# A feed-forward product split over two 64-row tiles of the tensor engine, with the halves exchanged after a drain

## The chip, the core and the metric

The kernel runs on one core of a Trainium2 chip. The core has five engines that run side by side, each with its own queue of instructions: TensorE (PE in the profile; its weight loads have a row of their own, PEld), VectorE (DVE), ScalarE (ACT), GpSimd (POOL) and SyncE (SP), which here starts the transfers. The metric is the time of one execution in device microseconds (us).

## What is computed

The reference is a block of two layers over 16 learned tokens and 256 input tokens with 1024 features. Each layer has a mixer (three branches: retention, a gated linear recurrence, and differential attention, with input projections, branch projections and an output projection) and then a feed-forward part with a short causal convolution. The change lies in the first product of the feed-forward part, `hn @ w_ffn_in`:

```python
def conv_ffn(hn, w_ffn_in, conv_w, conv_b, w_ffn_out, valid):
    u = jnp.where(valid[None, :, None], hn @ w_ffn_in, 0.0)
    up = jnp.pad(u, ((0, 0), (CONV_W - 1, 0), (0, 0)))
    c = conv_b + sum(conv_w[j] * up[:, j:j + l] for j in range(CONV_W))
    gate, val = jnp.split(c, 2, axis=-1)
    return (jax.nn.silu(gate) * val) @ w_ffn_out
```

`w_ffn_in` has 1024 rows and 5632 columns: 22 feature tiles of 128 for the gate and 22 for the value.

## The kernel before

**Layout.** Activations stand with features on the 128 partitions and tokens along the columns. A product takes a 128x128 tile of the weights as the loaded operand and all tokens as the moving one: 272 columns in the first layer, 258 in the second (`t0` is 0, then 14).

**Three products for one.** Each float32 operand is split into a rounded part and the rest, both of type `F32R` (the profile prints f32): `wh`, `wl` for weights, `hi`, `lo` for activations (tiles `xh`, `xl`). One tile of a product is `wh*hi + wh*lo + wl*hi`, lines 801, 802 and 803, each with a weight load of its own.

**`products` (line 780)** issues one pair of feature tiles. For `fi`, pair `j` is gate tile `j` and value tile `j+22`; `f` (0 or 1) says which of the two, and each accumulates in a PSUM bank of its own (`to[j, f]`). The eight row tiles `k` of the 1024 features are run through as k = 0 to 3, then 4 to 7, each with f = 0, then f = 1: 16 tiles, 48 matmuls. There are 22 such pairs in each of the two layers. The PSUM tile `main` has two buffers, so one pair can be emptied while the next is computed.

**Weights (`_Weights`, line 501)** come in chunks of eight tiles (512 KB): SP fetches `wraw` (3 buffers), ACT rounds it to `whi`, DVE takes the rest into `wlo` (4 buffers each), lines 524 to 526. A pair of `fi` uses two chunks, the first for k = 0 to 3, the second for k = 4 to 7. A chunk is asked for `LEAD` = 6 us ahead of its first use by the planner's clock.

**The planner.** Nothing is issued as it is written down. `plan.add` records an operation with its engine, an estimated cost and a key (a due time on `clock`, which the products advance); `_Plan.order` then simulates the engines and fixes the order of each queue by these costs, keys, dependencies and free buffers. In the code before, one planned operation is one tile (three matmuls). Real waits are semaphores set at the level of the instructions.

**Around the product.** The output projection `wo` runs before the first pair. While `fi` begins, the norm's factor is computed (a float32 matmul to `ms`, line 741, in pair 0), and the first four pairs are scaled by it when they are emptied (`evacuate`, DVE). From the fifth pair on (`DEFER`, `Norm.next`, line 750) the activations themselves carry the factor: the tiles for k < 4 go to a second set (`xs[2]`), those for k >= 4 are written again in place (`xs[1]`), with ACT writing `xh` and DVE writing `xl`. DVE and ACT also do the convolution of each pair (`two_b`), the gate and the split for the next product (`ghi`, `glo`). After the 22 pairs comes the second product `fo`.

**An existing place with 64 rows.** The attention scores (`da_head`, line 1176, tile `ds`) are float32 matmuls over 64 partitions: head part m = 0 on partitions 0 to 63, m = 1 on 64 to 127, issued in turn, into two PSUM banks.

```python
for q0, nk, at in tiles:
    for m in range(2):
        half = slice(64 * m, 64 * m + 64)
        nc.tensor.matmul(ss[m][:, at : at + nk], q[half, hd, q0 : q0 + P], k[half, hd, :nk], start=True, stop=True)
```

Of the kernel before, what the change touches and what calls it, by code (L numbers as in the profile page):

```python
# [25 lines left out]
KD = D // P  # L26
# [56 lines left out]
def _ktiles(name):  # L83
    return FK if name == "fo" else KD
# [462 lines left out]
def _trace(ctx, tc, plan, a, depth, probe):  # L547
    nc = tc.nc
    act = _Engine(plan, nc.scalar, "act", 0.094, 0.833e-3)
    dve = _Engine(plan, nc.vector, "dve", 0.068, 1.042e-3)  # L550
    pe = _Engine(plan, nc.tensor, "pe", 0.0, 4 / 2400)
# [12 lines left out]
    weights = _Weights(plan, wp, a["w"], act, dve, sync)  # L564
    serial = [0]

    def new(pool_, shape, dt, tag, bufs, name):
        serial[0] += 1
        return plan.tile(pool_, shape, dt, tag, bufs, f"{name}_{serial[0]}")

    def fixed(shape, name, dt=F32):
        return new(cp, shape, dt, name, 1, name)
# [86 lines left out]
    xs = [[fixed([P, KD // 2, T], f"x{n}{i}", F32R) for n in "hl"] for i in range(3)]  # L659

    def x_tile(k, folded):
        return tuple(t[:, k % 4, :] for t in xs[1 if k >= 4 else 2 if folded else 0])
# [113 lines left out]
    clock = [0.0]  # L776
# [3 lines left out]
    def products(xs, name, j, t0=0):  # L780

        if name in BASE or name == "fi":
            norm.next()
        if ahead:
            return ahead.pop()
        tiles = turns.pop(0)
        main = lambda: new(mp, [P, 2, 512], F32, "main", 2, "main")[:, :, t0:T]
        ps = {i: main() for i in sorted({x[1] for x in tiles})}
        to = {x: ps[x[0]][:, x[1], :] for x in {x[1::2] for x in tiles}}
        if (name, j) == ("fo", 3):  # L790

            to[j, 1] = main()[:, 1, :]
        cost = 3 * ((T - t0) / 2400 + 0.003)
        nk = _ktiles(name)
        for _, i, k, f in tiles:
            hi, lo = (x[:, t0:] for x in xs(k))
            plan.key = clock[0]
            wh, wl = weights.next()

            def run(o=to[i, f], wh=wh, wl=wl, hi=hi, lo=lo, first=k == 0, last=k == nk - 1):  # L800
                nc.tensor.matmul(o, wh, hi, start=first, stop=False)  # L801
                nc.tensor.matmul(o, wh, lo, start=False, stop=False)  # L802
                nc.tensor.matmul(o, wl, hi, start=False, stop=last)  # L803

            plan.main.append(plan.add("pe", run, cost, [to[i, f]], [wh, wl, hi, lo]))
            clock[0] += cost
        plan.key = clock[0] - 1.0
        if (name, j) == ("fo", 3):
            return [to[j, f] for f in range(2)]
        ahead.extend(ps[i] for i in ps if i != j)  # L810
        return ps[j]
# [64 lines left out]
    for li in range(depth):  # L876
# [4 lines left out]
        t0 = META - 2 if last else 0  # L881
# [453 lines left out]
        for name, j in ORDER:  # L1335
# [31 lines left out]
            if name in BASE:  # L1367
                lo = 0 if name in ("rk", "rv", "hf", "hi", "dk", "dv") else t0
                ps = products(lambda k: x_tile(k, norm.folded), name, j, lo)
                if name in ("rg", "hg", "m0", "m1", "m2"):  # L1370
                    if j == 0:
# [43 lines left out]
                else:  # L1415
# [6 lines left out]
                    if lo and j % 2:  # L1422
                        pool.memset(t[:, :, :lo], 0.0)
            elif name in ("b0", "b1", "b2"):
                ps = products(st["x" + name], name, j, t0)
                g = st["m" + name[1]][:, both, t0:]
                yy = block(f"y{j // 2}")[:, two, t0:]
# [10 lines left out]
            elif name == "wo":  # L1438
                hi, lo = st["yhi"], st["ylo"]
                ps = products(lambda k: (hi[k // 4][:, k % 4, :], lo[k // 4][:, k % 4, :]), name, j, t0)  # L1440
                tt(h[:, both, t0:], h[:, both, t0:], ps, ADD)
                if j == 0:
# [5 lines left out]
            elif name == "fi":  # L1448
                ps = products(lambda k: x_tile(k, norm.folded), name, j, t0)
# [9 lines left out]
                for f in range(2):  # L1459
                    ft = j + f * FK  # L1460
                    w = lambda i: small[:, S_CW + (li * 3 + i) * 2 * FK + ft : S_CW + (li * 3 + i) * 2 * FK + ft + 1]
# [12 lines left out]
            else:  # L1474
                hi, lo = st["ghi"], st["glo"]
                ps = products(lambda k: (hi[k // 4][:, k % 4, :], lo[k // 4][:, k % 4, :]), name, j)
# [34 lines left out]
```

## Time and profile before

| what | value |
|---|---|
| median of 2 runs | 1334.65 us (1334.08 to 1335.23) |
| the profiled execution | 1334.28 us, of which the span from first to last instruction is 1332.5 us |
| mean granted TensorE clock | 0.999 |
| matmuls, and as many weight loads | 11862 |
| matmuls of lines 801 to 803 into `main` from `xh`, `xl` | 2368 for each line |
| DVE, ACT busy | 72%, 61% of the span |

The profile is of one execution. Its rows give, for groups of instructions, the busy time, the mean duration of one, and what ended the idle time before them. Matmuls overlap in the pipeline, so the duration of one (some 290 ns) is longer than the distance from one start to the next; the distance is what a stream of matmuls costs. The end of a matmul is modelled.

### The profile page before, as it was taken

The numbers are of one execution on the slowest core, as the hardware profiler recorded it, in microseconds if no ns is written. First come the engines' busy times: TensorE is split into PE (matmuls) and PEld (weight loads), VectorE is DVE, ScalarE is ACT, GpSimd is POOL, SyncE is SP. The second block draws the span as 40 slices with busy tenths as digits, with TensorE's granted clock in tenths as the row PEclk, the third lists the DMA queues.
The fourth block names the chain that finished last, engine by engine and source line by source line (L and its number), as shares of the span: only waits on it lengthen the run. The fifth ranks groups of instructions, "written<-read, shape, count | busy, mean of one in ns | idle before, by whom it ended". The sixth has DMA issues, their size and how long they took to land.

```text
span 1332.5 us, 28912 instructions
## 1 busy us (share of the span) xinstructions
PE 1320.4 (99%) x11862; PEld 1292.5 (97%) x11862; DVE 961.9 (72%) x1628; ACT 813.2 (61%) x1371; POOL 84.2 (6%) x162
## 2 busy tenths in 40 slices
PE   9999999999999999999999999999999999999998
PEld 9999999999999999999999999999999999999986
DVE  7575777697676789886564757776985867898753
ACT  6747454756576567665446574557566775767643
POOL 5000000000010020000030000000011100200000
PEclk9999999999999999999999999999999999999999
DMA  7644543443544545555555545444445446466653
GB/s 269 192 142 156 164 160 128 139 147 127 175 143 157 176 152 174 183 174 176 177 177 180 161 151 167 161 128 144 143 152 169 143 156 203 143 206 189 196 186 109
DMA packets 60755, 219.07 MB, mean 164 GB/s; under 512 B 6864, under 2 KB 6992, under 8 KB 60624
## 3 DMA queue, kind: packets, MB, share of 16 engines
q1 hardware_dynamic: 60336, 216.71, 50.3%
q8 instruction: 93, 1.52, 0.5%
q10 hardware_dynamic: 288, 0.52, 0.1%
q14 instruction: 38, 0.31, 0.1%
HBM read 216.16 MB, written 1.05 MB: 163 GB/s over the span
## 4 chain that ended last, share of the span: by engine, by line
PE 94%; DVE 4%; issue 1%; DMA 1%; ACT 0%; SPq 0%; DVEq 0%
PE main L801 27%; PE main L802 27%; PE main L803 27%; PE fo L1311 2%; PE fo L1313 2%; PE fo L1312 2%; PE lev L992 1%; DVE two_b L496 1%; PE ds L1176 1%; DVE wlo L496 1%; PE ms L496 1%; PE do L496 1%; PE ro L496 1%; PE ho L496 1%; DVE xl L496 1%
## 5 line engine op out<-in xcount | busy, mean ns | idle before, releaser
L801 PE MATMUL main<-xh,whi 128*128 128x272 f32 (+1 forms) x2368 | 693.7, 293 | 1.8 <-ACT whi L496 1.1
L802 PE MATMUL main<-xl,whi 128*128 128x272 f32 (+1 forms) x2368 | 677.1, 286 | 2.4 <-DVE xl L496 2.4
L803 PE MATMUL main<-xh,wlo 128*128 128x272 f32 (+1 forms) x2368 | 677.0, 286 | 0.5 <-DVE wlo L496 0.4
L496 DVE TENSOR_TENSOR wlo<-wraw,whi 128x1024 fp32r<-128x1024 f32 (+1 forms) x406 | 496.4, 1228 | 204.5 <-ACT whi L496 201.3
L496 ACT ACTIVATE whi<-wraw 128x1024 fp32r<-128x1024 f32 (+1 forms) x406 | 426.3, 1052 | 235.4 <-PE main L802 165.1
L802 PEld LDWEIGHTS main<-xl,whi 128*128 128x128 f32 x2368 | 446.0, 188 | 3.5 <-DVE xl L496 3.0
L801 PEld LDWEIGHTS main<-xh,whi 128*128 128x128 f32 x2368 | 445.4, 188 | 3.5 <-ACT whi L496 1.3
L803 PEld LDWEIGHTS main<-xh,wlo 128*128 128x128 f32 x2368 | 445.0, 188 | 1.3 <-DVE wlo L496 1.3
L496 DVE SCALAR_TENSOR_TENSOR two_b<-main,small,two_b 128x256 f32<-128x256 f32 (+2 forms) x144 | 65.4, 487 | 29.3 <-ACT two_b L496 27.5
L496 POOL TENSOR_TENSOR y<-h,rstd 128x272 f32<-128x272 f32 x32 | 34.8, 1121 | 317.6 <-ACT rstd L496 317.6
L496 ACT ACTIVATE two_b<-main,small 128x272 f32<-128x272 f32 (+1 forms) x72 | 37.3, 566 | 27.2 <-PE main L803 27.2
L802 PE MATMUL main<-glo,whi 128*128 128x272 f32 x176 | 50.8, 289 | 0.0
L803 PE MATMUL main<-ghi,wlo 128*128 128x272 f32 x176 | 50.7, 288 | 0.0
L801 PE MATMUL main<-ghi,whi 128*128 128x272 f32 x176 | 50.6, 288 | 0.0
L496 ACT ACTIVATE vsrc<-main 128x544 f32<-128x544 f32 x24 | 15.0, 626 | 39.6 <-PE main L803 39.6
L496 POOL COPY tails<-vsrc 128x32 f32<-128x32 f32 x32 | 9.5, 312 | 462.0 <-ACT vsrc L496 462.0
L801 PE MATMUL main<-b0hi,whi 128*128 128x272 f32 (+1 forms) x128 | 38.1, 298 | 0.0
L801 PE MATMUL main<-b1hi,whi 128*128 128x272 f32 (+1 forms) x128 | 38.0, 297 | 0.0
L802 PE MATMUL main<-ylo,whi 128*128 128x272 f32 (+1 forms) x128 | 36.6, 286 | 0.0
L802 PE MATMUL main<-b2lo,whi 128*128 128x272 f32 (+1 forms) x128 | 36.6, 286 | 0.0
L802 PE MATMUL main<-b1lo,whi 128*128 128x272 f32 (+1 forms) x128 | 36.6, 286 | 0.0
L803 PE MATMUL main<-b0hi,wlo 128*128 128x272 f32 (+1 forms) x128 | 36.6, 286 | 0.0
(248 smaller groups left out, 1961.1 us busy)
## 6 DMA issues: line engine op xcount, KB each, us to landing
wraw<-in_w SPq DMA_DIRECT2D x402, 512.0 KB, 3.4
h<-in_h SPq DMA_DIRECT2D x4, 272.0 KB, 5.6
dec<-in_dec SPq DMA_DIRECT2D x2, 544.0 KB, 5.4
wraw<-in_w SPq DMA_DIRECT2D x4, 256.0 KB, 4.9
const<-in_const SPq DMA_DIRECT2D x1, 937.0 KB, 7.2
gain<-in_gl SPq DMA_DIRECT2D x1, 512.0 KB, 4.9
out<-y ACTq DMA_DIRECT2D x2, 256.0 KB, 2.8
out<-y SPq DMA_DIRECT2D x2, 256.0 KB, 2.7
```

The source lines that it names most:

```text
L496: self.plan.add(self.name, lambda: f(*args, **kw), cost, outs, ins, args[2] if method == "activation" else None)
L801: nc.tensor.matmul(o, wh, hi, start=first, stop=False)
L802: nc.tensor.matmul(o, wh, lo, start=False, stop=False)
L803: nc.tensor.matmul(o, wl, hi, start=False, stop=last)
L992: nc.tensor.matmul(o, keys, x, start=True, stop=True)
L1176: nc.tensor.matmul(ss[m][:, at : at + nk], q[half, hd, q0 : q0 + P], k[half, hd, :nk], start=True, stop=True)
L1311: nc.tensor.matmul(o, gh, wh, start=False, stop=False)
L1312: nc.tensor.matmul(o, gl, wh, start=False, stop=False)
L1313: nc.tensor.matmul(o, gh, wl, start=False, stop=end)
```

## The change

For `fi` alone, `products` takes a new path. Each 128-row product becomes two 64-row products, one on partitions 0 to 63 (m = 0) and one on 64 to 127 (m = 1), and these two go to different feature tiles: in the first turn m = 0 serves f = 0 while m = 1 serves f = 1, in the second turn the other way round. So each feature tile gets its lower half of the rows in one turn and the upper half in the other, and at any time the two row halves write different PSUM banks. A drain of the tensor engine stands between the turns. A pair of feature tiles has 96 matmuls instead of 48, each with a weight load, and one drain. Both weight chunks are used in both turns. A planned operation is now a quarter of the pair (four k of one turn: 24 matmuls, with 4 times the cost of a tile), so the sum of the planned costs of a pair is as before; the second chunk is asked for by the key of the second quarter, where it was that of the second half.

```diff
         nk = _ktiles(name)
+        if name == "fi":
+
+            operands = {}
+            for turn in range(2):
+                for half in range(2):
+                    ks = range(4 * half, 4 * half + 4)
+                    plan.key = clock[0]
+                    for k in ks:
+                        for f in range(2):
+                            if not turn:
+                                operands[k, f] = weights.next() + tuple(x[:, t0:] for x in xs(k))
+
+                    def run(turn=turn, half=half, ks=ks, operands=operands):
+                        if turn and not half:
+                            nc.tensor.drain()
+                        for k in ks:
+                            for q in range(3):
+                                for m in range(2):
+                                    f = (m + turn) % 2
+                                    wh, wl, hi, lo = (x[64 * m : 64 * m + 64] for x in operands[k, f])
+                                    w, x = ((wh, hi), (wh, lo), (wl, hi))[q]
+                                    nc.tensor.matmul(to[j, f], w, x, start=k == q == turn == 0, stop=k == KD - 1 and q == 2 and turn == 1)
+
+                    reads = [x for k in ks for f in range(2) for x in operands[k, f]]
+                    plan.main.append(plan.add("pe", run, 4 * cost, [to[j, f] for f in range(2)], reads))
+                    clock[0] += 4 * cost
+            plan.key = clock[0] - 1.0
+            return ps[j]
         for _, i, k, f in tiles:
```

## The prediction

> **What bounds the kernel now.** I read the head of the page first (busy shares, slices), then the chain that ended last.
>
> ```profile
> span 1332.5 us, 28912 instructions
> PE 1320.4 (99%) x11862; PEld 1292.5 (97%) x11862; DVE 961.9 (72%) x1628; ACT 813.2 (61%) x1371; POOL 84.2 (6%) x162
> ...
> PEclk9999999999999999999999999999999999999999
> ...
> PE 94%; DVE 4%; issue 1%; DMA 1%; ACT 0%; SPq 0%; DVEq 0%
> ```
>
> TensorE is the chain, at full clock in every slice. What is added on TensorE inside `fi` is paid in full unless another engine is the bound there. So the next view is the table of busy time by stretches, one stretch inside `fi` of each layer (columns: length, then busy us and count for each engine, clock, DMA share, GB/s).
>
> ```profile
> core 0: us, PE busy (x) PEld busy (x) DVE busy (x) ACT busy (x) POOL busy (x), PEclk, DMA share, GB/s
> ...
> 520.00:600.00 80.00, 80.00 (x641) 80.00 (x640) 66.53 (x111) 53.25 (x82) 0.00 (x0) 1.00 0.59 184
> ...
> 1180.00:1250.00 70.00, 70.00 (x589) 70.00 (x589) 59.48 (x101) 47.86 (x76) 0.00 (x0) 1.00 0.62 199
> ```
>
> Distance of matmuls: 80/641 = 0.125 us for 272 columns, 70/589 = 0.119 for 258. A pair of feature tiles is 48 of them: 6.0 and 5.7 us. DVE is busy 83% and 85%, ACT 67% and 68%: TensorE alone is the bound here.
>
> Third, the one place that works in 64 rows, the scores (line 1176): its rows, the timeline cut after its first two, first four and all eight matmuls, and the chain there and at a 128-row float32 stage with the same widths (`ro`).
>
> ```profile
> L1176 PE MATMUL ds<-dk,dq x128: 282/336/494, 291.5 to 1064.0; 64*128 64x272 f32 x64, 64*128 64x144 f32 x64
> ...
> 227.43 1.41 PE ro L496 x8
> ...
> 291.56 0.91 PE ds L1176 x8
> ```
>
> ```profile
> 291.28 0.29 PE L803 MATMUL main<-b0hi,wlo 128*128 128x272 f32 x1
> 291.49 0.50 PE L1176 MATMUL ds<-dk,dq 64*128 64x272 f32 x2
> ...
> 291.49 0.73 PE L1176 MATMUL ds<-dk,dq 64*128 64x272 f32 x4
> ...
> 291.49 0.97 PE L1176 MATMUL ds<-dk,dq 64*128 64x272 f32 x8
> ...
> 292.40 0.39 PE L801 MATMUL main<-b0hi,whi 128*128 128x272 f32 x1
> 292.63 0.28 PE L802 MATMUL main<-b0lo,whi 128*128 128x272 f32 x1
> ```
>
> Eight matmuls of 272 and 144 columns take 1.41 us one after the other (`ro`: 4 x 272 and 4 x 144 columns) but 0.91 in two row halves, entry included. The second two matmuls add 0.73 - 0.50 = 0.23 us together; the last four (two pairs of 144) add 0.24, so 0.12 a pair. So two row halves run side by side, loads included, and a pair costs what one float32 matmul of all 128 rows costs (1.41/1664 columns = 0.85 ns a column: 0.23 for 272, 0.12 for 144).
>
> Fourth, what waits inside `fi` now (fifth pair, when the activations change to the scaled ones), and the only drain of TensorE that is in the trace, at the end.
>
> ```profile
> 507.38 0.39 PE L802 MATMUL main<-xl,whi 128*128 128x272 f32 x1 [0.38 <-DVE xl L496]
> ...
> 1162.87 0.39 PE L802 MATMUL main<-xl,whi 128*128 128x258 f32 x1 [1.29 <-DVE xl L496]
> ```
>
> ```profile
> 1325.61 0.39 PE L1312 MATMUL fo<-whi,glo 128*128 128x512 f32 x1
> 1325.83 0.40 PE L1313 MATMUL fo<-wlo,ghi 128*128 128x512 f32 x1
> ```
>
> ```profile
> L1506 PEldq DRAIN x2: 13/2175/4337, 1321.9 to 1331.8; - x2
> ```
>
> **The change part by part.** All sums are against the profiled execution, 1334.28 us (span 1332.5 and 1.8 around it); the median 1334.65 is 0.03% above, which I neglect.
>
> *Twice the matmuls at half the rows.* `fi` has 2 x 22 x 48 = 2112 slots, 1056 of 0.125 us (132.0 us) and 1056 of 0.119 (125.6 us). Each becomes a pair of row halves. In float32 the pair costs what the full one does, so I take 0.125 and 0.119 again: 0 us. This is the disputed term, since no row shows type F32R at 64 rows. [...] At half of float32's pace a pair would cost 0.23/2 = 0.1155 and 0.1095 us: 0.0095 less in each of 2112 slots, -20 us, the lower end. The upper end is that the halves take turns, +257.6 us. I take 0: of the same type, full rows and row pair agree within 0.01 us.
>
> *Issue.* A pair of halves needs four instructions each 0.119 us. The level matmuls (line 992) went at 51 with their loads in 0.69 us on the chain, 0.0135 us for two instructions; enough. The 4268 more instructions at 64 bytes (1.83 MB for 28912 on the two instruction queues) are 0.27 MB of 219: 0 us, under other transfers.
>
> *The drain, 44 times.* Everything behind it on TensorE waits, the next loads too, which are otherwise fetched ahead. The drain at the end began at 1321.9 and took 4.337 us, to about 1326.26; the last matmul started at 1325.83 and its stream is 0.23 (distance of starts before it): the drain ends 0.2 after the stream. Then a load stands free: in the timeline the first `main` matmul after the scores has its successor 0.23 behind it instead of 0.125, so 0.105. With 0.03 for issue (an event on this queue took 0.051): 0.33 us. 44 x 0.33 = 14.5 us. Bounds: 0.20 (a change of row mode, below) gives 8.8, 0.50 (0.15 more for refilling the queue) gives 22.
>
> [...]
>
> *Change of row mode.* From 291.28 to 292.63 lie two full streams (0.25) and 0.70 of pairs (2 x 0.23, 2 x 0.12); the remaining 0.40 is entry and exit, 0.20 each. In `fi` this comes four times a layer (entry, around the float32 `ms`, exit): 8 x 0.20 = 1.6 us, bounds 0.8 and 2.4.
>
> *Coarser order, earlier second half.* The rows k >= 4 are wanted a quarter into the pair, 1.5 us earlier than now. It matters in the first pair (in layer 0 it begins at 479.2, right after the last `wo` matmul; the last `xl` ends at 482.4 in DVE's timeline; k = 7 is wanted 3.75 us into the pair, about 483, so 0) and in the fifth, where TensorE waits for DVE's `xl` already (0.54 and 1.45 us over the usual distance). There the wait grows by 1.5 and shrinks by the drains of four pairs before it (4 x 0.33 = 1.3), since DVE goes on during them; DVE's order may shift a little: +1 us for both layers, bounds 0 and 5.
>
> *Weights held longer.* The first chunk is free after 3/4 of the pair, not 1/2; two more fit in the four buffers, and the one that replaces it is wanted 1.25 pairs later (7 us). ACT 1.06 and DVE 1.23 us a chunk plus the transfer's 3.4 fit: 0 us. No transfer is added; SP asks for the second chunk 1.4 us earlier. Emptying PSUM is as before.
>
> Sum: 0 + 14.5 + 1.6 + 1.0 = 17.1 us; 1334.3 + 17.1 = 1351.4 us (+1.3%). Own range, with drains 0.20 to 0.50 and waits 0 to 5: 1345 to 1363.
>
> **Rivals.**
>
> *The row halves take turns (slower).* [...] Pairs cost 0.25 and 0.238: +257.6 + 17.1 gives 1609 us. It decides early: 2% is 26.7 us, 17.1 are spent, so 9.6/2112 = 0.0045 us more in a pair makes the kernel slower. A mild form, 0.005 to 0.025 more a pair (interlocks), gives 1362 to 1404.
>
> *The loads take turns (slower).* A load is 0.105 us whatever its rows; two in a row are 0.21 against a stream of 0.125. That gives (0.085 + 0.091) x 1056 = 186 us more, 1537 with the rest. Against it: the pairs of 144 columns went at 0.12, too short for two loads. [...]
>
> *The pairs get cheaper.* If F32R's excess over half of float32's pace belongs to full-row work, -20 us: 1334.3 + 17.1 - 20 = 1331, no change; with the cheapest drains 1325. It cannot pass 2%.
>
> *The drains are hidden.* Only where DVE is the bound, before the fifth pair: 2.6 us at most, counted above.
>
> **How the numbers follow.** Forecast (pairs at today's distance) 0.58; cheaper pairs 0.12; dearer by a little 0.10; turns of streams 0.14, of loads 0.06. The time is the forecast's, 1351 us. Range 1325 to 1374: the forecast, the cheaper pairs and half of the mild form, about 0.75 to 0.8. A measurement here tells a change from none at about 2%, 1308 to 1361. Slower: 0.14 + 0.06 + 0.10 + 0.03 (forecast with dear drains) = 0.33. Faster: 0.02 for what I don't see. Same: 0.65.
>
> **What will show it.** In the changed profile, matmuls of `main` in `fi` should be 64 rows, starts in twos some 0.01 apart, twos every 0.125 and 0.119 us: 192 matmuls and loads per pair within 6.3 and 6.0 us. A drain's gap should be 0.33 from the end of a stream to the next. Twos at 0.25, or at 0.21, name the rivals; at 0.115, the third. The fifth pair's wait should stay under 3 us. I am wrong if F32R in row halves is not like float32, or if a drain costs over 0.5 us.

## The result and the profile after

The changed kernel takes 1352.19 us (median of 2 runs, 1351.82 to 1352.56) against 1334.65: a ratio of 1.0131, 95% interval 1.0088 to 1.0175. The profiled execution took 1352.56 us with a span of 1350.8.

The head of the page of the changed kernel, its chain, and the groups of the new line (816 in its own numbering; lines 801 to 803 of before are now 829 to 831):

```profile
span 1350.8 us, 33186 instructions
...
PE 1335.4 (99%) x13974; PEld 1295.7 (96%) x13974; DVE 958.7 (71%) x1628; ACT 811.7 (60%) x1371; POOL 83.1 (6%) x162
...
PEclk9999999999999999999999999999999999999999
...
PE 94%; DVE 4%; issue 1%; DMA 1%; ACT 1%; SPq 0%; DVEq 0%; ACTq 0%
...
L816 PE MATMUL main<-xh,whi 64*128 64x272 f32 (+1 forms) x1408 | 209.8, 288 | 3.7
...
L816 PEld LDWEIGHTS main<-xh,whi 64*128 64x128 f32 x1408 | 136.6, 184 | 13.6 <-issue 13.3
```

There are 2112 matmuls and 2112 loads more, the clock is full, the chain is TensorE as before. The last row points at the loss: 13.3 us in which the loads of `xh,whi` wait for "issue", that is for nothing that the profile counts as work. A drain is such a thing. It has no row among the groups, but the view of its line has it, once for all 44 and once for a window with a single one (shortest, median and longest in ns, then first and last start):

```profile
L809 PEldq DRAIN  x44: 523/1477/1547, 483.6 to 1277.0; - x44
...
L809 PEldq DRAIN  x1: 1542/1542/1542, 547.4 to 547.4; - x1
```

Its 1.5 us are not its price: this one begins to wait at 547.4, while the matmuls in front of it go on starting until 548.6. The price is in the timeline of TensorE around it (start, duration, then the group; each row is two matmuls, one for each row half):

```profile
548.47 0.29 PE L816 MATMUL main<-xl,whi 64*128 64x272 f32 x2
548.60 0.29 PE L816 MATMUL main<-xh,wlo 64*128 64x272 f32 x2
548.97 0.40 PE L816 MATMUL main<-xh,whi 64*128 64x272 f32 x2
549.20 0.30 PE L816 MATMUL main<-xl,whi 64*128 64x272 f32 x2
549.32 0.30 PE L816 MATMUL main<-xh,wlo 64*128 64x272 f32 x2
```

Twos of row halves follow each other every 0.125 us, the distance of the full rows before. From 548.60 to 549.20 are 0.60 us in which two streams of 0.125 run; the other 0.35 is the drain. (By the single records the drain ends 0.19 us after the last stream, the next load starts 0.05 later, and the stream, reckoned back from the one behind it, some 0.105 after that. In the stream a load starts some 0.12 ahead of its matmul, at 548.48 for the one at 548.60; the first load behind the drain starts at 548.97, as its matmul is listed to.)

A stretch inside `fi` of layer 0, first the changed kernel (columns as in the prediction), then, in its own fence and with the column of PE alone, the kernel of the first experiment, which has the row halves but no drain:

```profile
520.00:600.00 80.00, 78.95 (x1210) 76.17 (x1206) 60.91 (x103) 48.72 (x78) 0.00 (x0) 1.00 0.57 171
```

```profile
520.00:600.00 80.00, 80.00 (x1280) 1.00 0.58 181
```

1280 halves in 80 us are 640 twos, where 641 full matmuls stood before. With the drain they are 605.

All experiments are read by one number besides their time: the distance from the first matmul of a pair of feature tiles to that of the next, as the mean over pairs 8 to 21 of each layer, from the starts in the trace. In pairs 2 to 6 it is longer than that, where TensorE waits; what these five pairs have over the steady distance, both layers together, is called the waits of the first pairs. (Before, 0.2 us of it is the norm's `ms`, which in layer 1 stands just ahead of the second pair, so differences are good to some 0.2 us.) The times are medians of 2 to 11 executions, but blocks of six and of twelve were executed once each. The ratios below are to executions of the kernel before that went with the experiment, whose median was 1333.69 to 1333.80 us.

| kernel | time, us | pair in layer 0, us | pair in layer 1, us |
|---|---|---|---|
| before | 1334.65 | 6.013 | 5.720 |
| changed | 1352.19 | 6.366 | 6.091 |
| row halves, no exchange, no drain | 1339.86 | 6.013 | 5.733 |
| full rows, one drain a pair | 1348.02 | 6.388 | 6.113 |
| order of planning alone, full rows | 1337.86 | 6.013 | 5.733 |
| two drains together | 1355.3 | 6.446 | 6.169 |
| two drains apart | 1366.19 | 6.740 | 6.470 |
| one matmul a pair in row halves | 1348.63 | 6.400 | 6.116 |
| row halves in blocks of 3 | 1352.73 | 6.384 | 6.100 |
| row halves in blocks of 6 | 1367.58 | 6.724 | 6.449 |
| row halves in blocks of 12 | 1489.77 | 9.630 | 9.234 |
| one row half alone | 1513.77 | 6.01 to 10.88 | 5.73 to 10.32 |
| before, with tiles of their own | 1334.61 | 6.020 | 5.760 |
| changed, with tiles of their own | 1350.81 | 6.384 | 6.090 |

### The profile page after: what moved, and what is told of

Same layout as the page of the kernel before. It is cut to its first block, busy times and chain, and to the rows that moved or that the text cites. A ratio compares the mean times of both kernels' runs of the same rounds, so it can differ in the third digit from the quotient of the medians.

```text
span 1350.8 us, 33186 instructions
## 1 busy us (share of the span) xinstructions
PE 1335.4 (99%) x13974; PEld 1295.7 (96%) x13974; DVE 958.7 (71%) x1628; ACT 811.7 (60%) x1371; POOL 83.1 (6%) x162
## 4 chain that ended last, share of the span: by engine, by line
PE 94%; DVE 4%; issue 1%; DMA 1%; ACT 1%; SPq 0%; DVEq 0%; ACTq 0%
PE main L829 21%; PE main L830 21%; PE main L831 21%; PE main L816 17%; PE fo L1339 2%; PE fo L1341 2%; PE fo L1340 1%; PE lev L1020 1%; DVE wlo L496 1%; PE ds L1204 1%; PE ms L496 1%; PE do L496 1%; DVE two_b L496 1%; PE ro L496 1%; PE ho L496 1%
## 5 line engine op out<-in xcount | busy, mean ns | idle before, releaser
L829 PE MATMUL main<-xh,whi 128*128 128x272 f32 (+1 forms) x1664 | 492.7, 296 | 1.0 <-issue 0.6
L830 PE MATMUL main<-xl,whi 128*128 128x272 f32 (+1 forms) x1664 | 476.6, 286 | 0.7 <-DVE xl L496 0.7
L831 PE MATMUL main<-xh,wlo 128*128 128x272 f32 (+1 forms) x1664 | 476.5, 286 | 0.6 <-DVE wlo L496 0.6
L830 PEld LDWEIGHTS main<-xl,whi 128*128 128x128 f32 x1664 | 313.6, 188 | 1.4 <-DVE xl L496 0.9
L816 PE MATMUL main<-xh,whi 64*128 64x272 f32 (+1 forms) x1408 | 209.8, 288 | 3.7
L816 PE MATMUL main<-xl,whi 64*128 64x272 f32 (+1 forms) x1408 | 205.4, 282 | 1.8 <-DVE xl L496 1.7
L816 PE MATMUL main<-xh,wlo 64*128 64x272 f32 (+1 forms) x1408 | 205.5, 282 | 0.1
L816 PEld LDWEIGHTS main<-xh,whi 64*128 64x128 f32 x1408 | 136.6, 184 | 13.6 <-issue 13.3
L816 PEld LDWEIGHTS main<-xl,whi 64*128 64x128 f32 x1408 | 136.8, 185 | 2.9 <-DVE xl L496 2.9
L816 PEld LDWEIGHTS main<-xh,wlo 64*128 64x128 f32 x1408 | 136.7, 184 | 0.5 <-DVE wlo L496 0.5
```

The source lines that it names most:

```text
L816: nc.tensor.matmul(to[j, f], w, x, start=k == q == turn == 0, stop=k == KD - 1 and q == 2 and turn == 1)
```

## The experiments

**Row halves without the drain.** The exchange is left out with it, so that no two halves write one bank; each feature tile then gets the same half of the rows twice.

```diff
-                        if turn and not half:
-                            nc.tensor.drain()
...
-                                    f = (m + turn) % 2
+                                    f = m
```

> The changed kernel without the drain; so that none is needed, the halves are not exchanged: row half 0 always serves the first feature tile and row half 1 the second, in both turns (the sums of the product are therefore over the wrong halves; count, order and size of matmuls and loads are as in the changed kernel). Theory (the row halves are free, the drain is the cost): the 44 drains go, only mode changes of 1.6 us and some 1 us of waits stay over the kernel before: 1337 us. Rival (half of the loss or more sits in the doubled matmuls and loads, not in the drain): 1345 us or more.

Measured 1339.86 us, 1.0044 (1.0029 to 1.0059) times before. The pair of feature tiles takes 6.013 and 5.733 us, exactly what full rows take in the same order of planning (third run), and within 0.013 of the kernel before. So twice the matmuls and twice the loads cost nothing, and drain and exchange together cost 6.366 - 6.013 = 0.353 and 6.091 - 5.733 = 0.358 us. The total is 3 us above my 1337: the waits of the first pairs are 7.8 us here, 4.8 more than before, where I had counted 1. The next run but one says what they are. Some 1.5 of the 7.8 us are of another kind: in the fifth pair of layer 1 the granted clock of the profiled execution falls to a half for 3.4 us (16 twos at 0.215 instead of 0.119 us; the columns are length, PE busy and count, granted clock, DMA share, GB/s):

```profile
1166.00:1168.00 2.00, 2.00 (x22) 0.63 0.01 2
1168.00:1170.00 2.00, 2.00 (x22) 0.52 0.00 0
1170.00:1172.00 2.00, 2.00 (x38) 1.00 0.20 61
```

**Full rows with a drain.** `mid` is true for k = 4 and the first feature tile of each pair of `fi`, so the drain stands in the middle of the pair.

```diff
+                if mid:
+                    nc.tensor.drain()
                 nc.tensor.matmul(o, wh, hi, start=first, stop=False)
```

> The kernel before, with full rows, and one drain in the middle of each pair of the first feed-forward product (44 drains). Theory: a drain costs what the trace of the changed kernel shows, 0.19 us of waiting, 0.05 of issue and 0.105 of a load that stands free, 0.35 us: 44 times 15.4, so 1350 us. Rival (the drain is dear only with 64-row tiles, where two streams and two loads start again): 0.25 us or less each, 1346 us or less.

Measured 1348.02 us, 1.0104 (1.0089 to 1.0119). One drain in its timeline:

```profile
533.38 0.28 PE L805 MATMUL main<-xh,wlo 128*128 128x272 f32 x1
533.76 0.39 PE L803 MATMUL main<-xh,whi 128*128 128x272 f32 x1
533.99 0.29 PE L804 MATMUL main<-xl,whi 128*128 128x272 f32 x1
```

Here too 0.61 us pass where two streams of 0.125 run. A drain in full rows costs 0.374 and 0.393 us a pair, a little more than between row halves: its price does not come from the 64-row tiles. 44 of them are 16.9 us, yet the kernel lost some 14. The difference is in the waits of the first pairs: 2.98 us before, 0.5 us here. DVE goes on while TensorE drains: in the changed kernel it is busy in the whole 0.24 us before the first matmul behind a drain (495.82 to 496.06 and 548.73 to 548.97).

**The order of planning alone.** Full rows; first feature tile in the first turn, second in the second; no drain.

```diff
-                        if turn and not half:
-                            nc.tensor.drain()
...
-                                for m in range(2):
-                                    f = (m + turn) % 2
-                                    wh, wl, hi, lo = (x[64 * m : 64 * m + 64] for x in operands[k, f])
...
+                                wh, wl, hi, lo = operands[k, turn]
...
+                                nc.tensor.matmul(to[j, turn], w, x, start=k == q == 0, stop=k == KD - 1 and q == 2)
```

> The changed kernel's planning alone: four planned operations per pair, chunks held over both turns, the second half of the rows wanted a quarter into the pair; but full rows, the first feature tile in the first turn, the second in the second, and no drain. Theory: only the fifth pair's wait grows, 1 us in all: 1335.5 us. Rival (coarser order and weights held longer cost a good part of the 17.5 us): 1340 us or more.

Measured 1337.86 us, 1.0031 (1.002 to 1.0042): between the two theories. The steady pairs are as long as before in layer 0 and 0.013 us longer in layer 1, but the waits of the first pairs are 6.8 us, against 3.0 before. TensorE's timeline of this kernel, its rows with a wait in the fourth and fifth pair of layer 0 (in brackets the idle time and what ended it):

```profile
499.77 0.40 PE L812 MATMUL main<-xh,wlo 128*128 128x272 f32 x1 [0.96 <-DVE wlo L496]
506.14 0.39 PE L812 MATMUL main<-xl,whi 128*128 128x272 f32 x1 [0.59 <-DVE xl L496]
507.18 0.39 PE L812 MATMUL main<-xl,whi 128*128 128x272 f32 x1 [0.40 <-DVE xl L496]
```

and the same rows of the changed kernel:

```profile
507.54 0.40 PE L816 MATMUL main<-xl,whi 64*128 64x272 f32 x2 [0.24 <-DVE xl L496]
...
508.58 0.39 PE L816 MATMUL main<-xl,whi 64*128 64x272 f32 x2 [0.40 <-DVE xl L496]
```

Besides the scaled activations (`xl`), the second chunk of the weights (`wlo`) comes late: the wait stands at its first use, which is now a quarter into the pair. Of the 3.8 us that the order adds, the fourth pair, which had no wait before, has 2.6 and the fifth 2.0, while the other three have 0.8 less. In the changed kernel the drains of the first pairs give DVE the time: its waits are 4.1 us, 1.1 more than before. With row halves and this order the waits are 6.3 us without a drain (7.8 less the 1.5 of the clock), 4.1 with one in each pair and 1.5 with two (below). So the order costs 3.8 us alone and 1.1 together with the drains.

**A second drain behind the first.**

```diff
                             nc.tensor.drain()
+                            nc.tensor.drain()
```

> The changed kernel with a second drain right behind each drain. Theory (the price is waiting for the array to empty and a load that could not be fetched ahead): the second finds the array empty and costs its issue only, 0.05 us: 44 times 2.2 us, 1354.5 us. Rival (a fixed price for each drain instruction): 0.37 us more each, 1368.5 us.

Measured 1355.3 us, 1.0165 (1.0148 to 1.0182); the second drain costs 0.080 and 0.078 a pair. A drain instruction that follows another costs 0.08; the other 0.27 of the first one's 0.35, more than three quarters, go with the waiting for the last matmuls and the load behind (0.19 and 0.105 by the records above). My 0.05 was a little low.

**A second drain a quarter later.**

```diff
-                        if turn and not half:
+                        if turn:
```

> The changed kernel with a drain ahead of both quarters of the second turn, so two per pair, apart from each other (88 in all). Theory: the second costs as much as the first, 0.37 us: 44 times 16.3 us, 1368.5 us. Rival (the first drain pays for something done once per pair, as the exchange of the halves or a wait on another engine): under 1360 us.

Measured 1366.19 us, 1.0245 (1.0229 to 1.026). The second drain costs 0.374 and 0.379 a pair, as much as the first, though no halves are exchanged at it: the price is that of the drain and not of the exchange. 44 of them are 16.6 us; the total rose by 14, and again the rest comes out of the waits of the first pairs (1.5 us here, 4.1 in the changed kernel).

**One matmul of each pair in row halves.** The kernel before; for k = 4 and the first feature tile, the product `wl*hi` is cut into two halves that go to different feature tiles (half of it thus to the wrong one).

```diff
+                if mid:
+                    for m in range(2):
+                        half = slice(64 * m, 64 * m + 64)
+                        nc.tensor.matmul(to[j, m], wl[half], hi[half], start=False, stop=False)
+                    return
                 nc.tensor.matmul(o, wl, hi, start=False, stop=last)
```

> The kernel before, with one of the 48 full-row matmuls of each pair in the first feed-forward product replaced by two 64-row matmuls side by side, one into each feature tile's bank (this puts half of that product into the wrong feature tile); no drain. Theory: one entry into the 64-row mode and one exit per pair, 0.2 us each: 44 times 0.4 = 17.6 us, 1352 us. Rival (the gaps at the scores belong to float32, and a change of row mode alone costs little): 1336 to 1340 us.

Measured 1348.63 us, 1.0112 (1.0097 to 1.0127). An entry and an exit together cost 0.387 and 0.396 a pair, 0.19 to 0.20 for each change, as at the scores. The total is 3 us under my 1352, for the reason found above. A change of row mode twice is as dear as one drain (0.374 and 0.393 in full rows); whether a change is a drain, this run does not show.

**The halves in blocks of twelve, six and three.** The change issues the halves in turn. Here each quarter is issued as twelve matmuls of one half and then twelve of the other; then six and six; then three and three.

```diff
-                        for k in ks:
-                            for q in range(3):
-                                for m in range(2):
+                        for m in range(2):
+                            for k in ks:
+                                for q in range(3):
```

> The changed kernel with the halves not issued in turn: in each quarter twelve matmuls of row half 0, then twelve of row half 1. Theory (matmuls start in the order of issue, so two halves run side by side only when they stand next to each other in the queue): each block of twelve takes 12 times 0.125 us and only the ends of blocks overlap, 6 to 7 per pair: 257.6 us more less 44 x 6.5 x 0.12 = 35, so about 1575 us. Rival (the engine finds the other half's matmuls in its window): 1352 to 1400 us.

Measured 1489.77 us: between the two theories, so neither was right. Side by side the pair would take 6.366; at 9.630 it needs 3.264 / 0.125 = 26 slots more than the 48, that is 74 for 96 matmuls, so 22 of them still ran beside one of the other half. There are seven changes of block in a pair without a drain between: three each. The timeline at one change shows the three, between matmuls that run alone:

```profile
540.38 0.28 PE L816 MATMUL main<-xh,wlo 64*128 64x272 f32 x1
540.39 0.41 PE L816 MATMUL main<-xh,whi 64*128 64x272 f32 x2
540.62 0.30 PE L816 MATMUL main<-xl,whi 64*128 64x272 f32 x2
540.75 0.30 PE L816 MATMUL main<-xh,wlo 64*128 64x272 f32 x2
540.87 0.28 PE L816 MATMUL main<-xh,whi 64*128 64x272 f32 x1
```

So I formed another theory from these counts, that matmuls start in order but the engine holds about three more per half ready, and tried the other sizes.

> As before it, in blocks of six (two k of row half 0, then two of row half 1). Theory (about three at each change of block, 15 changes per pair): 96 - 41 = 55 slots of 0.125 us, 0.9 us more per pair than side by side: about 1390 us. Rival (one per change of block): 96 - 15 = 81 slots, 4.0 us more per pair: about 1530 us.

> The changed kernel with the halves issued in blocks of three: for each k the three products of row half 0, then the three of row half 1. From the run with blocks of twelve (9.63 us a pair of feature tiles, where 48 slots side by side and a drain take 6.37): of 96 matmuls some 22 ran side by side with one of the other half, about 3 at each change of block. Theory (the engine starts matmuls in order but holds about three more per half ready): blocks of three run side by side in full, 6.4 us a pair, 1352 to 1357 us. Rival (only neighbours in the queue overlap, one per change of block): 16 blocks with one overlap each per quarter pair of k, 96 - 31 = 65 slots, 8.1 us plus the drain, about 1445 us.

Measured 1367.58 and 1352.73 us. Blocks of three run side by side in full (0.017 and 0.008 us a pair more), as expected. Blocks of six were expected at 1390, which came from counting 2.75 at a change instead of 3. With three at each of 15 changes they leave 96 - 45 = 51 slots, 3 lost, 0.375 us; measured 0.358 in both layers. A count of three fits all three sizes, but for six it was set after the result; what in the engine makes it three, and whether it holds matmuls ready at all, no run here shows.

**One row half alone.** The third run, against which the cut is shown; rows 64 to 127 are left out.

```diff
-                                wh, wl, hi, lo = operands[k, turn]
+                                wh, wl, hi, lo = (x[:64] for x in operands[k, turn])
```

> The order of e5, with rows 0 to 63 alone: 48 matmuls of 64 rows per pair and nothing at the same time in the other half (it leaves out half of the sums). Theory (F32R's distance of 0.125 and 0.119 us belongs to the type and the columns, not to the number of rows that stream): as e5 with 1.6 us of mode changes, 1337 us. Rival (the excess over half of float32's pace comes from 128 rows streaming at once): 0.1155 and 0.1095 us, 20 us less, 1317 us.

Measured 1513.77 us, and for a reason that neither theory had. The first pairs run as expected: 6.01 us for the second, so 0.125 us for a lone half, which speaks for the theory. Then the clock falls. The wait just before it, and stretches of this kernel in layer 0 (length, PE busy and count, granted clock, DMA share, GB/s):

```profile
501.37 0.39 PE L812 MATMUL main<-xh,wlo 64*128 64x272 f32 x1 [1.13 <-DVE wlo L496]
```

```profile
495.00:500.00 5.00, 5.00 (x42) 1.00 0.62 212
500.00:505.00 5.00, 3.87 (x24) 0.81 0.42 120
505.00:510.00 5.00, 5.00 (x24) 0.50 0.57 201
560.00:600.00 40.00, 40.00 (x178) 0.50 0.28 92
...
704.00:710.00 6.00, 6.00 (x34) 0.67 0.45 139
```

From 503.1 to 707.9 us the granted clock is 0.50, though TensorE is busy without a gap (40.00 of 40.00 us in the stretch from 560), and it comes back about 4 us after the product with full rows (`fo`) has begun. The same happens in layer 1 (1250.7 to 1445.2). In both layers the fall comes in the fourth pair, 1.8 us after the end of the wait for `wlo` (1.13 us here); the same order with full rows waits at the same place (0.96 us, above), and there the clock stays. So in this run a stream over 64 rows alone lost the clock behind that wait, from 1.00 to 0.50, and did not win it back in 200 us. The two halves side by side lost it once too, in the first experiment behind the waits of the fifth pair of layer 1, but won it back in 3.4 us. Up to its wait the lone half had run for 22 us at full clock; whether the fall needs the wait was not tried.

**Tiles of their own for the scaled activations.** For k >= 4 they are written over the unscaled ones; here they get two free slots instead, once in the kernel before and once in the changed one.

```diff
     def x_tile(k, folded):
+        if folded and k >= 4 and norm.own:
+            return tuple(t[:, k % 4, :] for t in norm.own)
...
+            if self.ffn:
+                self.own = [slot4("own", F32R) for _ in range(2)]
```

> The kernel before (full rows, no drain); the scaled activations for k >= 4 of the feed-forward part get tiles of their own instead of being written over the unscaled ones. Theory (the wait of 3 us in all in the fifth and sixth pairs of both layers comes from writing in place, which puts DVE's four writes late): most of it goes, 1331.5 to 1333 us, faster than both. Rival (DVE is the bound there whatever the tiles): 1334 us, no change.

> The changed kernel with the same tiles of their own for k >= 4. Theory (its waits of 4 us in the fourth and fifth pairs come from the short time between the last read of k >= 4 and the next pair's first): 2 to 4 us less, 1348 to 1350 us. Rival (DVE is the bound there): 1352 us.

Measured 1334.61 us, 1.0007 (0.9998 to 1.0016) times before: no change, the rival; the waits of the first pairs are 3.0 us with and without. And 1350.81 us, 1.0128 (1.0112 to 1.0143) times before for the changed kernel, which without the tiles had 1.0131: no difference that is clear of noise. In the traces its waits go from 4.1 to 2.5 us, 1.6 less where I had expected 2 to 4, and the steady pairs of layer 0 grow by 0.018 us. So writing in place is not what makes TensorE wait in the kernel before; in the changed one, by one trace of each, some 1.6 of the 4.1 us come from it. That DVE's load in these pairs is, as the rival says, was not tested further; for it speaks that DVE has no idle time around the wait of the fifth pair in the kernel before (columns as in the prediction, DVE the third of the busy ones):

```profile
505.00:512.00 7.00, 6.62 (x52) 6.23 (x51) 7.00 (x13) 5.03 (x9) 0.00 (x0) 1.00 0.39 124
```

## Why the prediction was right, point by point

The forecast was 1351 us in a range of 1325 to 1374, by pairs at today's distance, drains, changes of row mode and small waits. The span grew by 18.3 us, of which the steady pairs, the first pairs and the rest give:

| term | forecast, us | measured, us |
|---|---|---|
| twice the matmuls and loads | 0 | 0.0 (6.013 and 5.733 with full rows and with halves) |
| order of planning in the steady pairs | not in the sum | 0.3 (22 x 0.000 + 22 x 0.013) |
| 44 drains | 14.5 | 15.6 (22 x 0.353 + 22 x 0.358) |
| waits in the first pairs | 1.0 | 1.1 (4.1 - 3.0) |
| changes of row mode | 1.6 | 1.3 (what is left) |
| sum | 17.1 | 18.3 |

*The pairs.* That two F32R halves run as one full matmul was the disputed term. It was taken from float32, whose row pair and full row agreed, and it held to 0.001 us a pair against full rows in the same order. Both rivals with turns are ruled out by the run without the drain, and the cheaper pairs too: full rows, two halves and one half alone (before the clock fell) all stream at 0.125 us. In these runs F32R's pace did not depend on the number of rows. The lower end of the range stood on half of float32's pace for a pair of halves (0.1155 and 0.1095 us, -20 us); no run shows such a pace, for halves or for full rows. Nor does one show the 0.005 to 0.025 us of interlocks behind the upper end: the halves take 0.000 us a pair more than full rows in the same order. The loads that were to take turns are listed at 187 ns for 64 rows (`ds`) and 188 for 128 (`main`) in the kernel before, 128 columns each; twice as many of them cost nothing. The lone half at a granted clock of 0.50 took 10.88/48 = 0.227 us, 1.81 times 0.125 and not twice, so a part of the 0.125 does not go with the clock; what it is, no run here shows.

*The drain.* Forecast 0.33, measured 0.353 to 0.358: 0.19 of waiting, 0.05 to the next load (the step that I had at 0.03), 0.105 of a load, and 0.01 until the second half starts too. The waiting, read from the one drain of TensorE in the trace of before, at its end, was right to 0.01. The 0.15 more for refilling the queue, in the upper bound of 0.50, is a term that no run shows: a drain by itself cost 0.353 to 0.393 us with all that followed it. Whether the exchange needs a whole drain, or something cheaper would do, was not tried.

*The waits.* The sum was right, and its parts nearly so. For the two layers I had 3.0 us of growth, 2.6 of relief by the drains and 0.6 for a shift in DVE's order; alone, the order costs 3.8 us, and the drains give 2.7 of it back. But the growth was put in the wrong place: I had it all in the fifth pair and at `xl`, and 2.6 us of it came in the fourth, at the second chunk's `wlo`. That the sum came out all the same is in part luck. "7 us: 0 us" was right for the buffers that the first chunk holds; the step that I had not seen is when the second chunk is first wanted.

*The change of row mode.* 0.20 each, from the scores; the run made for it gives 0.19 to 0.20.

So the change does what it says and gains nothing by it: the array streams no faster when it is cut in two (0.125 us for two halves as for one full matmul of 272 columns), and each exchange of the halves costs a drain of 0.35 us.

## What to carry to other kernels

Cutting a full contraction into row halves moved no work off the array (640 twos in 80 us, where 641 full matmuls ran). Halves side by side paid where half the rows stood empty, as at the scores (0.91 us for eight matmuls, where eight of the same widths over full rows take 1.41). Read a price from the steady stretch of a loop, not from the total: here 16.9 us of drains in one run showed as 14, because another engine, DVE, went on during them (waits of the first pairs 0.5 us, against 2.98). And when the operations of a loop are regrouped, ask of each operand not only how long it is held but when it is first wanted.

## What the runs showed of the hardware that I had not expected

- 64 rows alone, in the run of one row half, ran for 204.8 us (194.6 in layer 1) at a granted clock of 0.50, and the clock came back some 4 us after full rows had begun. PE is busy 100% of the stretches shown; the clock stayed at 0.50 all the same. Two halves side by side, in the run without the drain, came back from such a fall (0.52 in its lowest stretch) after 3.4 us.
- Halves need not be issued in turn: in layer 0 blocks of three take 6.384 us a pair, against 6.366 in turn, blocks of six 6.724 (0.36 more) and blocks of twelve 9.630 (3.3 more).
- A drain right behind another cost 0.08 us (two drains together), one by itself 0.35 to 0.39 (in row halves, in full rows, and a quarter later).
